# Fewer ones-matmuls in the RMS statistics, and residual adds as two wide VectorE operations

## The chip, the cores and the metric

The kernel runs on all eight cores of one Trainium2 chip, with the same program on each core and different tokens. The metric is device time in microseconds (us) of the slowest core. A run's time is some 2 us above its slowest core's span, so times are compared with times and spans with spans. The chip has two dies of four cores. In some executions of any version one die, or both, gets a lower TensorE clock. Such runs are called slow.

## The reference, cut to what matters

```python
def rmsnorm(x, g):
    xf = x.astype(jnp.float32)
    y = xf * lax.rsqrt(jnp.mean(xf * xf, axis=-1, keepdims=True) + EPS)
    return (y * g.astype(jnp.float32)).astype(x.dtype)

for i in range(DEPTH):                       # 4 layers
    h = rmsnorm(x, g[0]); x = x + 0.5 * rmsnorm(swiglu(h, ...), g[1])
    h = rmsnorm(x, g[2]); m = conv_mixer(h) if i % 2 == 0 else pool_mixer(h)
    x = x + rmsnorm(m, g[3])
    h = rmsnorm(x, g[4]); x = x + 0.5 * rmsnorm(swiglu(h, ...), g[5])
```

D_MODEL is 1024. Norms 0, 2 and 4 of a layer are prenorms, and norms 1, 3 and 5 are postnorms, each followed by a residual add.

## The kernel before

A core takes its 2112 tokens in two passes of three tiles (`t`) of 352 tokens. Model channels lie on the 128 partitions, so a tile is 8 chunks of 128 x 352. The mean over channels is therefore a sum across partitions. The kernel gets it by multiplying the squares with a 128 x 128 matrix of ones, 8 matmuls into one PSUM bank (PSUM is the memory, in eight banks here, that TensorE writes its sums to):

```python
def norm_stats(t, srcs, skeys, scale=None):
    b = t % 2
    v = S.vt(stat=True)                      # the one statistics bank
    for c in range(NCH):
        srcs(c, b)                           # ACT: sq[b][:, c, :] = square, bf16
    for hf in range(2):
        def f(pe, hf=hf):
            for c in range(4 * hf, 4 * hf + 4):
                mm = pe.matmul(B(v)[:, 0:TS], lhsT=ones_bf[:], rhs=sq[b][:, c, :], start=(c == 0), stop=(c == NCH - 1))
            return mm
        S.op("pe", f, 4 * MM, ...)
    S.op("act", [... Ln in the bank, then Exp(-0.5 *) into rr[b] ...])

def postnorm(l, n, t, half):
    ...
    for c in range(NCH):                     # scaling, in place, on VectorE
        S.op("dve", ... acc = acc * gain * rr ..., c_dve(TS) + 0.02, ...)
    for c in range(NCH):                     # residual add
        eng = "pool" if c < 4 else "dve"
        S.op(eng, ... x = x + acc ..., c_pool(TS) if eng == "pool" else c_dve(TS), ...)
```

`S.op` does not run anything. A list scheduler orders all operations beforehand: the third argument is a cost in us from a small table (`c_dve`, `c_act`, `c_pool`, `MM`), and each engine later executes its own list strictly in that order. If the table is wrong, an engine can stand before an operation whose input is late while others behind it are ready.

Of the kernel before, what the change touches and what calls it, by code (L numbers as in the profile page):

```python
# [12 lines left out]
D = 1024  # L13
# [378 lines left out]
def build_program():  # L392
# [19 lines left out]
    x = [sb(f"x{t}", [128, NCH, TS], F32) for t in range(NTILE)]  # L412
    h = [sb(f"h{t}", [128, NCH, TS], BF16) for t in range(NTILE)]
    acc = [sb(f"acc{t}", [128, NCH, ACW], F32) for t in range(NTILE)]
    sq = [sb(f"sq{i}", [128, NCH, TS], BF16) for i in range(2)]
    gt = [sb(f"gt{i}", [128, GRP, TS], BF16) for i in range(2)]
    ring = sb("ring", [128, RU, 1024], BF16)
    wdn = [sb(f"wdn{i}", [128, GRP * 128], BF16) for i in range(NCH)]
# [26 lines left out]
    def B(v):  # L445
        return banks[S.vbank[v]]
# [37 lines left out]
            st["ld"] += 1  # L484
        return units

    def norm_stats(t, srcs, skeys, scale=None):

        b = t % 2
        v = S.vt(stat=True)  # L490
        for c in range(NCH):
            srcs(c, b)
        for hf in range(2):
            def f(pe, hf=hf):
                for c in range(4 * hf, 4 * hf + 4):
                    mm = pe.matmul(B(v)[:, 0:TS], lhsT=ones_bf[:], rhs=sq[b][:, c, :], start=(c == 0), stop=(c == NCH - 1))
                return mm
            S.op("pe", f, 4 * MM, reads=["ones"] + [("sq", b, c) for c in range(4 * hf, 4 * hf + 4)], vts=[v],
                 prio=P_STAT, margin=0.6)
        S.op("act", [lambda a: a.activation(out=B(v)[:, 0:TS], in_=B(v)[:, 0:TS], func=AF.Ln, scale=1.0 / D, bias=epst[:, 0:1]),  # L500
                     lambda a: a.activation(out=rr[b][:], in_=B(v)[:, 0:TS], func=AF.Exp, scale=-0.5)],
             2 * c_act(TS) + 0.15, reads=["eps"], writes=[("rr", b)], vts=[v], prio=P_CH, margin=0.2, tbl="lnexp", wvt=True)

    def sq_sbuf(t, src, key, off):
        def s(c, b):
            S.op("act", lambda a: a.activation(out=sq[b][:, c, :], in_=src[:, c, off:off + TS], func=AF.Square),
                 c_act(TS, True), reads=[(key, t, c)], writes=[("sq", b, c)], prio=P_CH, margin=0.1)
        return s

    def prenorm(l, n, t, to_u=False):  # L510
        b = t % 2
        norm_stats(t, sq_sbuf(t, x[t], "x", 0), None)
        for c in range(NCH):
            g = gcol(l, n, c)
            dst = acc[t][:, c, PAD:ACW] if to_u else h[t][:, c, :]
            S.op("dve", lambda v, c=c, g=g, dst=dst: v.scalar_tensor_tensor(
                out=dst, in0=x[t][:, c, :], scalar=params[:, g:g + 1], in1=rr[b][:], op0=ALU.mult, op1=ALU.mult),
                c_dve(TS) + 0.02, reads=[("x", t, c), ("rr", b), "params"], writes=[("acc" if to_u else "h", t, c)],
                prio=P_CH, margin=0.1)

    def postnorm(l, n, t, half):
        b = t % 2
        pt = params_h if half else params
        pk = "params_h" if half else "params"
        for c in range(NCH):
            g = gcol(l, n, c)
            S.op("dve", lambda v, c=c, g=g: v.scalar_tensor_tensor(
                out=acc[t][:, c, PAD:ACW], in0=acc[t][:, c, PAD:ACW], scalar=pt[:, g:g + 1], in1=rr[b][:],
                op0=ALU.mult, op1=ALU.mult),
                c_dve(TS) + 0.02, reads=[("acc", t, c), ("rr", b), pk], writes=[("acc", t, c)], prio=P_CH, margin=0.1)  # L530
        for c in range(NCH):
            eng = "pool" if c < 4 else "dve"
            S.op(eng, lambda v, c=c: v.tensor_tensor(out=x[t][:, c, :], in0=x[t][:, c, :], in1=acc[t][:, c, PAD:ACW], op=ALU.add),
                 c_pool(TS) if eng == "pool" else c_dve(TS), reads=[("acc", t, c), ("x", t, c)], writes=[("x", t, c)],
                 prio=P_CH, margin=0.1)

    def ffn_tile(g, t, slots, finish):
        u = st["u"] % 2
        st["u"] += 1
        for jj in range(GRP):  # L540
            q = st["q"] % 3
            st["q"] += 1
            va, vb = S.vt(), S.vt()
            for v, un in ((va, slots[jj][0]), (vb, slots[jj][1])):
                def fa(pe, v=v, un=un):
                    for k in range(NCH):
                        mm = pe.matmul(B(v)[:, 0:TS], lhsT=ring[:, un, k * 128:(k + 1) * 128], rhs=h[t][:, k, :],
                                       start=(k == 0), stop=(k == NCH - 1))
                    return mm
                S.op("pe", fa, NCH * MM, reads=[("h", t, k) for k in range(NCH)] + [("ru", un)], vts=[v])  # L550
            S.op("act", lambda a, va=va, q=q: a.activation(out=sa[q][:], in_=B(va)[:, 0:TS], func=AF.Silu),
                 c_act(TS), writes=[("sa", q)], vts=[va], prio=P_EV, tbl="silu")
            S.op("dve", lambda v_, vb=vb, q=q, u=u, jj=jj: v_.tensor_tensor(
                out=gt[u][:, jj, :], in0=B(vb)[:, 0:TS], in1=sa[q][:], op=ALU.mult),
                c_dve(TS), reads=[("sa", q)], writes=[("g", u, jj)], vts=[vb], prio=P_EV)
        for dc in range(NCH):
            v = S.vt()

            def fo(pe, v=v, u=u, dc=dc):
                for jj in range(GRP):  # L560
                    mm = pe.matmul(B(v)[:, 0:TS], lhsT=wdn[dc][:, jj * 128:(jj + 1) * 128], rhs=gt[u][:, jj, :],
                                   start=(jj == 0), stop=(jj == GRP - 1))
                return mm
            S.op("pe", fo, GRP * MM, reads=[("g", u, jj) for jj in range(GRP)] + [("wdn", dc)], vts=[v])
            if g == 0:
                S.op("act", lambda a, v=v, dc=dc: a.activation(out=acc[t][:, dc, PAD:ACW], in_=B(v)[:, 0:TS], func=AF.Copy),
                     c_act(TS), writes=[("acc", t, dc)], vts=[v], prio=P_EV)
            else:
                S.op("dve", lambda v_, v=v, dc=dc: v_.tensor_tensor(
                    out=acc[t][:, dc, PAD:ACW], in0=B(v)[:, 0:TS], in1=acc[t][:, dc, PAD:ACW], op=ALU.add),  # L570
                    c_dve(TS), reads=[("acc", t, dc)], writes=[("acc", t, dc)], vts=[v], prio=P_EV)
        if g == 1:
            norm_stats(t, sq_sbuf(t, acc[t], "acc", PAD), None)
            finish(t)

    def ffn(f, finish):
        for g in range(2):
            slots = [load_units(wab[f, g * GRP + jj], 2) for jj in range(GRP)]
            for dc in range(NCH):
                S.op("pool", lambda p_, dc=dc, g=g: p_.dma_start(out=wdn[dc][:], in_=wd[f, g, dc]), 0.55,  # L580
                     writes=[("wdn", dc)], dma=f"wdn{dc}", nbytes=GRP * 128 * 256, prio=-1)
            for t in range(NTILE):
                ffn_tile(g, t, slots, finish)

    def s6(ap):
        return ap.rearrange("p (s k) -> p s k", k=6)
# [4 lines left out]
    def conv_tile(j, p, t, slots, finish):  # L591
# [61 lines left out]
                S.op("sp", lambda e: e.dma_start(out=cs_p[j], in_=convh[:, j].rearrange("p a b -> p (a b)")), 0.06,  # L653
                     reads=[("convh", j, c) for c in range(NCH)], dma="cs_p", nbytes=8192, final=True)

        def sqs(dc, b):
            v = S.vt()

            def fw(pe):
                for cc in range(NCH):  # L660
                    mm = pe.matmul(B(v)[:, 0:TS], lhsT=wdn[dc][:, cc * 128:(cc + 1) * 128], rhs=gt[u][:, cc, :],
                                   start=(cc == 0), stop=(cc == NCH - 1))
                return mm
            gk = [("g", u, cc) for cc in range(NCH)]
            S.op("pe", fw, NCH * MM, reads=gk + [("wdn", dc)], vts=[v])
            S.op("act", lambda a: a.activation(out=acc[t][:, dc, PAD:ACW], in_=B(v)[:, 0:TS], func=AF.Copy), c_act(TS),
                 writes=[("acc", t, dc)], vts=[v], prio=P_EV)
            S.op("act", lambda a: a.activation(out=sq[b][:, dc, :], in_=B(v)[:, 0:TS], func=AF.Square), c_act(TS),
                 writes=[("sq", b, dc)], vts=[v], prio=P_EV)
        norm_stats(t, sqs, None)  # L670
        finish(t)

    def conv_mixer(l, p, finish):
# [20 lines left out]
    def pool_tile(l, p, t, finish):  # L694
# [70 lines left out]
                        in1=Sv[:, c * NSS:(c + 1) * NSS, 15:19], op0=ALU.mult, op1=ALU.subtract), 0.2,  # L765
                        reads=[("wins", g % 2), "S0", "S1"], writes=[("h", t, c)], prio=P_CH)

        def sqs(dc, b):
            v = S.vt()
            g = dc // 2  # L770

            def fp(pe):
                for cc in range(2):
# [5 lines left out]
            sc = 240 + j * 8 + dc  # L779
            S.op("act", lambda a: a.activation(out=A[:, dc, PAD:ACW], in_=B(v)[:, 0:TS], func=AF.Copy, scale=params[:, sc:sc + 1]),  # L780
                 c_act(TS) + 0.09, reads=["params"], writes=[("acc", t, dc)], vts=[v], prio=P_EV)
            S.op("act", lambda a: a.activation(out=sq[b][:, dc, :], in_=B(v)[:, 0:TS], func=AF.Square, scale=params[:, sc:sc + 1]),
                 c_act(TS) + 0.09, reads=["params"], writes=[("sq", b, dc)], vts=[v], prio=P_EV)
        norm_stats(t, sqs, None)
        finish(t)

    def win_view(a0, w):
# [20 lines left out]
    for p in range(NPASS):  # L808
        for l in range(NLAYER):
# [3 lines left out]

            def fin1(t, l=l, p=p, conv=conv):
                postnorm(l, 1, t, True)
                prenorm(l, 2, t, to_u=not conv)
                if not conv:
                    pool_tile(l, p, t, fin2)

            def fin2(t, l=l):  # L820
                postnorm(l, 3, t, False)
                prenorm(l, 4, t)

            def fin3(t, l=l, p=p):
                postnorm(l, 5, t, True)
# [5 lines left out]
                        load_x(p + 1, t)  # L831
                        prenorm(0, 0, t)

            ffn(2 * l, fin1)
            if conv:
                conv_mixer(l, p, fin2)
            ffn(2 * l + 1, fin3)

    S.run()
    S.finish()  # L840
# [82 lines left out]
```

## Time and profile before

| | before |
|---|---|
| fast runs | 4532.48, 4532.67, 4533.64 us |
| TensorE busy | 4459.6 us, 98% |
| VectorE, ScalarE, GpSimd busy | 42%, 40%, 18% |
| matmuls | 29,760, of them 1152 with ones |

The views that matter are quoted in the prediction below. A line of the groups reads: source line, engine, operation, output<-inputs, shapes, count, then busy us and mean ns of one, then the idle time in front of it and what ended that. A line of busy time by stretch reads: stretch, its length, then busy us and count (x) for TensorE, its weight loads, VectorE, ScalarE and GpSimd, then granted clock, DMA share and GB/s. A line of the waits reads: who waited for whom, total us, times, longest.

In the names, `sq`, `sqf` and `sqs` are squares and their sums, `rr` is the result of the Exp, that is the norm's factor, and `h` is the output of a prenorm, which the next matmuls read.

To tell pace from loss I use one measure throughout: **lost** = length of a stretch minus its matmuls x 0.1491 us, the spacing in a steady stretch.

### The profile page before, as it was taken

The numbers are of one execution on the slowest core, as the hardware profiler recorded it, in microseconds if no ns is written. First come the engines' busy times: TensorE is split into PE (matmuls) and PEld (weight loads), VectorE is DVE, ScalarE is ACT, GpSimd is POOL, SyncE is SP. The second block draws the span as 40 slices with busy tenths as digits, with TensorE's granted clock in tenths as the row PEclk, the third lists the DMA queues.
The fourth block names the chain that finished last, engine by engine and source line by source line (L and its number), as shares of the span: only waits on it lengthen the run. The fifth ranks groups of instructions, "written<-read, shape, count | busy, mean of one in ns | idle before, by whom it ended". The sixth has DMA issues, their size and how long they took to land.

```text
span 4532.7 us, 70376 instructions; the slowest of 8 cores (4528.3 to 4532.7 us)
## 1 busy us (share of the span) xinstructions
PE 4459.6 (98%) x29760; PEld 2911.6 (64%) x29760; DVE 1926.4 (42%) x3581; ACT 1832.7 (40%) x3527; POOL 824.2 (18%) x1329
## 2 busy tenths in 40 slices
PE   7999999999999999999999999999999999999998
PEld 4666666666666666666666666666666666666665
DVE  2255151753336424174333642427342463342834
ACT  3345242553334424264333443426443444343632
POOL 1122020321112211032111221113111121111311
PEclk9999999999999999999999999999999999999999
DMA  6445444424444544443553444444444434444440
GB/s 126 73 75 89 77 77 77 68 44 69 65 77 68 89 77 77 77 77 52 102 108 65 68 84 77 77 77 77 74 68 65 66 56 77 74 77 77 82 74 39
DMA packets 104571, 340.10 MB, mean 75 GB/s; under 512 B 11840, under 2 KB 13248, under 8 KB 104256
## 3 DMA queue, kind: packets, MB, share of 16 engines
q0 software_dynamic: 97776, 312.52, 43.2%
q1 hardware_dynamic: 6480, 23.09, 1.6%
q8 instruction: 234, 3.83, 0.3%
q14 instruction: 81, 0.66, 0.1%
HBM read 636.49 MB, written 11.55 MB: 143 GB/s over the span
## 4 chain that ended last, share of the span: by engine, by line
PE 93%; DVE 4%; ACT 2%; DMA 1%; issue 0%; SPq 0%; DVEq 0%
PE ps L350 93%; DVE acc L350 2%; DMA x<-x_in 1%; ACT sq L350 1%; DVE x L350 1%; DVE gt L350 0%; ACT L350 0%; DVE h L350 0%; ACT ps L350 0%; ACT sa L350 0%; ACT rr L350 0%; DVE scr L350 0%; ACT acc L350 0%; SPq L350 0%; DVEq L368 0%
## 5 line engine op out<-in xcount | busy, mean ns | idle before, releaser
L350 PE MATMUL ps<-h,ring 128*128 128x352 bf16 x19200 | 2924.4, 313 | 0.0
L350 PEld LDWEIGHTS ps<-h,ring 128*128 128x128 bf16 x19200 | 1881.4, 98 | 990.7 <-DVE h L350 0.5
L350 PE MATMUL ps<-gt,wdn 128*128 128x352 bf16 x9216 | 1406.6, 313 | 1.1 <-DVE gt L350 0.8
L350 DVE TENSOR_TENSOR gt<-ps,sa 128x352 bf16<-128x352 f32 x1056 | 550.2, 522 | 1929.7 <-PE ps L350 1893.1
L350 PEld LDWEIGHTS ps<-gt,wdn 128*128 128x128 bf16 x9216 | 901.2, 98 | 475.6 <-DVE gt L350 2.9
L350 ACT ACTIVATE sa<-ps 128x352 f32<-128x352 f32 x1152 | 531.8, 462 | 1387.6 <-PE ps L350 1333.1
L350 POOL DMA_DIRECT2D ring<-wab x352 | 189.2, 539 | 1758.9 <-PE ps L350 1751.5
L350 POOL TENSOR_TENSOR x<-x,acc 128x352 f32<-128x352 f32 x288 | 323.6, 1146 | 979.9 <-DVE acc L350 979.2
L350 ACT ACTIVATE acc<-ps 128x352 f32<-128x352 f32 x480 | 222.6, 464 | 494.3 <-PE ps L350 494.3
L350 DVE TENSOR_TENSOR acc<-ps,acc 128x352 f32<-128x352 f32 x384 | 200.7, 523 | 454.3 <-PE ps L350 453.8
L350 ACT ACTIVATE sq<-acc 128x352 bf16<-128x352 f32 x384 | 190.7, 497 | 450.1 <-DVE acc L350 449.9
L350 ACT ACTIVATE sq<-x 128x352 bf16<-128x352 f32 x576 | 271.5, 494 | 190.5 <-DVE x L350 83.4
L350 DVE SCALAR_TENSOR_TENSOR acc<-acc,params_h,rr 128x352 f32<-128x352 f32 x384 | 312.1, 861 | 28.5 <-ACT rr L350 28.5
L350 ACT ACT_TABLE_LOAD x235 | 301.5, 1283 | 5.7 <-PEq L393 1.1
L350 PE MATMUL ps<-sq,ones_bf 128*128 128x352 bf16 x1152 | 223.0, 318 | 58.4 <-ACT sq L350 39.9
L350 DVE SCALAR_TENSOR_TENSOR h<-x,params_sb,rr 128x352 bf16<-128x352 f32 x480 | 254.6, 578 | 51.3 <-ACT rr L350 50.8
L350 POOL DMA_DIRECT2D wdn<-wd x256 | 135.7, 533 | 327.1 <-PE ps L350 327.1
L350 PEld LDWEIGHTS ps<-sq,ones_bf 128*128 128x128 bf16 x1152 | 110.5, 99 | 130.3 <-ACT sq L350 50.4
L350 DVE SCALAR_TENSOR_TENSOR acc<-acc,params_sb,rr 128x352 f32<-128x352 f32 x192 | 150.1, 827 | 7.7 <-ACT rr L350 7.7
L350 DVE TENSOR_TENSOR x<-x,acc 128x352 f32<-128x352 f32 x288 | 137.9, 512 | 0.0
L350 DVE SCALAR_TENSOR_TENSOR scr<-scr,params_sb 128x352 f32<-128x352 f32 (+1 forms) x192 | 117.8, 614 | 25.2 <-ACT scr L350 23.5
L350 ACT ACTIVATE scr<-scr,params_sb 128x352 f32<-128x352 f32 (+1 forms) x96 | 57.0, 594 | 120.4 <-DVE scr L350 120.4
(39 smaller groups left out, 833.4 us busy)
## 6 DMA issues: line engine op xcount, KB each, us to landing
ring<-wab POOLq DMA_DIRECT2D x352, 512.0 KB, 11.3
wdn<-wd POOLq DMA_DIRECT2D x256, 352.0 KB, 15.8
ring<-wci POOLq DMA_DIRECT2D x29, 768.0 KB, 11.4
x<-x_in SPq DMA_DIRECT2D x12, 704.0 KB, 12.4
y_o<-x SPq DMA_DIRECT2D x12, 704.0 KB, 4.0
wdn<-wco POOLq DMA_DIRECT2D x32, 256.0 KB, 12.9
scr<-spool SPq DMA_DIRECT2D x4, 608.0 KB, 13.0
ps_s<-scr SPq DMA_DIRECT2D x4, 608.0 KB, 2.9
```

The source lines that it names most:

```text
L350: ins = attr(*a, **k)
```

## The change

The intent is to take matmuls off the bound engine. Squares are kept in fp32 and VectorE adds 8 chunks to 2, so that two ones-matmuls do. It is used wherever the statistic can come later without harm: in all norms of the convolution layers, and in norms 0 and 5 of the pooling layers. The four middle norms of the pooling layers keep eight matmuls. Separately, the residual adds leave GpSimd and become two adds of 1408 columns on VectorE.

```diff
-    sq = [sb(f"sq{i}", [128, NCH, TS], BF16) for i in range(2)]
+    sqf = sb("sqf", [128, NCH, TS], F32)         # one buffer; sq[0], sq[1] become views of it
+    sqs2 = sb("sqs", [128, 2, TS], BF16)
...
+    def norm_stats_pre(t, srcs):
+        for hf in range(2):
+            srcs(hf)                             # ACT: one square of 4 chunks, 1408 columns
+            o = 4 * hf
+            S.op("dve", ... sqf[:, o:o + 2] += sqf[:, o + 2:o + 4] ..., c_dve(2 * TS), ...)
+        S.op("dve", ... sqs2 = sqf[:, 0:2] + sqf[:, 4:6] ..., c_dve(2 * TS), ...)
+        def f(pe):
+            for c in range(2):
+                mm = pe.matmul(B(v)[:, 0:TS], lhsT=ones_bf[:], rhs=sqs2[:, c, :], start=(c == 0), stop=(c == 1))
+            return mm
...  # postnorm
-        for c in range(NCH):
-            eng = "pool" if c < 4 else "dve"
-            S.op(eng, ... x[t][:, c, :] + acc[t][:, c, PAD:ACW] ...)
+        for hf in range(2):
+            o = 4 * hf
+            ... four scalings of acc ...
+            S.op("dve", ... x[t][:, o:o + 4, :] + acc[t][:, o:o + 4, PAD:ACW] ..., c_dve(4 * TS), ...)
...
-                prenorm(l, 2, t, to_u=not conv)
+                prenorm(l, 2, t, to_u=not conv, pre=conv)
...
-            ffn(2 * l + 1, fin3)
+            last = p == NPASS - 1 and l == NLAYER - 1
+            ffn(2 * l + 1, fin3, lambda t, last=last: not (last and t == NTILE - 1))
```

## The prediction

> **What bounds the kernel now.** I read the busy table first, then the groups of instructions, then busy time by stretch, then the waits of TensorE, then the order of time inside one troubled stretch. The busy table and the groups come first:
>
> ```profile
> PE 4459.6 (98%) x29760; PEld 2911.6 (64%) x29760; DVE 1926.4 (42%) x3581; ACT 1832.7 (40%) x3527; POOL 824.2 (18%) x1329
> ...
> L350 POOL TENSOR_TENSOR x<-x,acc 128x352 f32<-128x352 f32 x288 | 323.6, 1146 | 979.9 <-DVE acc L350 979.2
> ...
> L350 DVE SCALAR_TENSOR_TENSOR acc<-acc,params_h,rr 128x352 f32<-128x352 f32 x384 | 312.1, 861 | 28.5 <-ACT rr L350 28.5
> ...
> L350 PE MATMUL ps<-sq,ones_bf 128*128 128x352 bf16 x1152 | 223.0, 318 | 58.4 <-ACT sq L350 39.9
> ...
> L350 DVE SCALAR_TENSOR_TENSOR h<-x,params_sb,rr 128x352 bf16<-128x352 f32 x480 | 254.6, 578 | 51.3 <-ACT rr L350 50.8
> ```
>
> TensorE is busy 98% of the span, everything else under half. 1152 of its 29,760 matmuls are the ones-matmuls of the norm statistics (144 norms of 8), so they cost the path directly. The mean of 318 ns is of a pipelined instruction; the price is the spacing, which I take from busy time by stretch (columns: stretch, length, then busy time and count for each engine, then granted clock, DMA share, GB/s):
>
> ```profile
> 256.00:622.00 366.00, 365.93 (x2454) 240.05 (x2455) 167.59 (x322) 151.01 (x296) 73.68 (x142) 1.00 0.46 73
> 943.00:1372.00 429.00, 428.98 (x2877) 281.21 (x2875) 153.98 (x286) 160.50 (x305) 62.94 (x91) 1.00 0.41 66
> 1977.00:2053.00 76.00, 69.80 (x459) 43.99 (x457) 63.96 (x106) 52.58 (x100) 32.36 (x40) 1.00 0.72 115
> 2053.00:2063.00 10.00, 9.34 (x52) 5.66 (x53) 7.42 (x13) 6.72 (x10) 1.95 (x2) 0.83 0.01 2
> 3092.00:3170.00 78.00, 71.45 (x474) 45.60 (x471) 64.80 (x107) 51.98 (x100) 33.08 (x41) 1.00 0.69 112
> ```
>
> 429.00 / 2877 = 0.1491 us per matmul in a steady stretch, and 366 / 2454 gives the same. 29,760 x 0.1491 = 4437 us, so 96 us of the 4532.7 are not matmuls at full pace. I can place them. Up to 38 us only 34 matmuls are done (33 us lost, a little more while the clock recovers); the end, from 4517 us, holds 7 (15 us lost). The pooling layers, two in each of two passes, show as four stretches of 76 to 78 us, which lose most of the rest: 76 - 459 x 0.1491 = 7.6 us here, 7.3 to 7.8 in the others, 30 us in all, and about 1.6 us more each while the clock is down after the last gap (52 matmuls in 10 us at a granted 0.83), some 6 us. So 36 us are pooling-layer stalls; some 10 us are scattered over the rest. In them VectorE is busy 64 of 76 us.
>
> TensorE's own waits name the cause:
>
> ```profile
> PE ps L350 <- ACT sq L350: 39.9, 23, 11.4
> PE ps L350 <- ACT rr L350: 18.4, 13, 3.1
> PE ps L350 <- DVE gt L350: 0.8, 2, 0.6
> ```
>
> It hardly ever waits for anything but ones-matmuls: for their squares, or for the one statistics bank that the previous Exp still reads. The kernel fixes its instruction order beforehand from a table of costs; it puts a ones-matmul where that table says its input is ready, and other matmuls were free to take the place. So such a wait is mostly an error of the table. The order of time in the second pooling stretch shows the error:
>
> ```profile
> 1978.47 6.75 DVE L350 SCALAR_TENSOR_TENSOR acc<-acc,params_sb,rr 128x352 f32<-128x352 f32 x8 [0.52 <-ACT rr L350]
> ...
> 1995.38 1.38 DVE L350 TENSOR_TENSOR x<-x,acc 128x352 f32<-128x352 f32 x3
> 1996.69 1.56 DVE L350 SCALAR_TENSOR_TENSOR h<-x,params_sb,rr 128x352 bf16<-128x352 f32 x3
> ```
>
> ```profile
> 1979.14 4.71 POOL L350 TENSOR_TENSOR x<-x,acc 128x352 f32<-128x352 f32 x4 [0.92 <-DVE acc L350]
> ```
>
> Eight scalings of acc take 6.75 us while GpSimd adds beside them; undisturbed ones follow each other every (1.56 - 0.57) / 2 = 0.49 us, so eight should take 4.0. The table knows 0.54 each and no such slowing.
>
> **What the Trainium skill says.** "TensorE: Matmul & The Clock Gate", "Wait — 56ns, not 53.3ns?": a warm matmul of N columns costs N / 2.4 ns + 2.5, for 352 columns 149.2 ns. The trace's 149.1 agrees. "SBUF — State Buffer", "SBUF: two separate sides": VectorE with two SBUF inputs and a GpSimd operation that reads SBUF exclude each other on a shared port pair for the whole instruction. The 6.75 us for eight agree. "VectorE: DVE Perf Modes", "The TRN2 errata": an fp32 two-tensor add takes (N + 151) / 0.96 ns, for 352 columns 524; the trace has 512. "ScalarE: Activation LUTs", "What ACT_TABLE_LOAD costs": an activation with immediates takes 186 + 0.833 N ns and successive ones overlap by 93; 479 for 352, and the trace has 494 to 497 for the squares.
>
> **The change, part by part.** Statistics first. Which norms change: in the convolution layers all 6, in the pooling layers the first and the last; 8 per pair of layers, times 2 pairs, 2 passes and 3 tiles makes 96, and the last tile of all is left out: 95. Each goes from 8 ones-matmuls to 2, so 95 x 6 = 570 matmuls go. All lie in streams where TensorE is full, so **570 x 0.1491 = 85.0 us** come off the path. Nothing of what replaces them is on TensorE.
>
> What it adds to VectorE: three fp32 adds of 704 columns. An undisturbed add of 352 repeats every (1.38 - 0.51) / 2 = 0.435 us, that is 352 / 0.96 GHz = 0.367 plus 0.068; for 704 columns 0.80, estimated. 95 x 3 x 0.80 = 228 us, beside the matmuls. ScalarE gets cheaper where it squares from SBUF: two wide instructions of about 1.36 us by the skill's formula for eight at a spacing near 0.39. The statistic comes some 2 us later than before (a wide square and two adds after the last chunk instead of one small square). In the convolution layers a tile has the time of other tiles' matmuls to finish, 264 x 0.149 = 39 us each, so I count 0 for that.
>
> Residual adds. Per postnorm (72 of them) VectorE before: 6.75 + 4 x 0.435 = 8.5 us, with GpSimd's 4.7 beside it. After: 8 x 0.49 + 2 x (1408 / 960 + 0.068) = 3.9 + 3.1 = 7.0 us, nothing on GpSimd. So the move takes 1.5 us of VectorE away per postnorm. In total: 72 x 1.5 = 108 less, 228 more, so VectorE goes from 1926 to about 2045 us, 45%.
>
> What this is worth on the path: the pooling layers keep their 8 ones-matmuls in the middle norms, so only the residual part reaches those stretches. It takes about 6 x 1.5 = 9 us of VectorE work out of 76, and the table's 8.2 us (0.54 each plus two adds of 1.62, and small gaps) is then above the real 7.0 instead of below the real 8.5. Waits that are errors of the table should mostly go. GpSimd's windowed sums still disturb VectorE there, so not all: I take **22 of the 36 us**.
>
> Start: tile 2's statistics become one step later in TensorE's order, not two halves with the first blocking; 0 to 4 us, I take **2**. End: the last tile keeps the old statistics, then 7.1 us of VectorE replace 8.5: **1.3**.
>
> Sum: 4532.7 - 85.0 - 22 - 2 - 1.3 = 4422 us.
>
> **Rivals.** (a) Only the matmuls count: the pooling waits are real shortage, or new order errors replace the old. Then 4532.7 - 85 - 1 = 4447 us, just inside 2%. For it: VectorE is still the busiest engine there. Against: each gap ends at a ones-matmul while plenty of other matmuls follow at once. (b) VectorE becomes the bound: adds of 1.5 us and 228 us of new work delay evictions, TensorE waits for banks, and the saving is eaten: 4470 to 4530. For it: the longest new operation outlasts one matmul group of 8 (1.2 us). Against: seven banks for it, and VectorE at 42% overall. (c) All pooling stalls go, and the start gains 4: 4532.7 - 85 - 36 - 5 = 4407. (d) The longer statistics chain stalls TensorE in the convolution layers, 1 us for each of 95 norms: the gain shrinks to about 4510; the 39 us of slack per tile speak against it.
>
> **Range and chances.** The 85 us are a count and nearly sure. What is open is 0 to 36 us of stalls, with (b) and (d) unlikely. So 4407 to 4443. The 2% line is 4442; only near-total failure of the second part crosses it: faster 0.87, same 0.12, slower 0.01.
>
> **What would show it.** TensorE with 29,190 matmuls, 582 of them ones-matmuls, still 0.149 us apart; acc scalings at a mean near 0.57 us instead of 0.83 to 0.86; no GpSimd adds of x; adds of 704 columns near 0.87 us each, of 1408 near 1.6; TensorE's waits for squares and Exp down from 58 us to about 30, with most of that at the start; pooling stretches losing 2 to 4 us each. It is wrong if the pooling stretches still lose 7 us, if TensorE waits for VectorE's sums in the convolution layers, or if its matmul spacing changes.

## The result, and the profile after

| | before | after |
|---|---|---|
| fast runs, us | 4532.48, 4532.67, 4533.64 | 4414.52, 4415.19 |
| slow runs, us | 4747.26 | 4499.20, 4754.77 |
| median of all four, us | 4533.16 | 4457.19 |
| span of the profiled run, us | 4532.7 | 4412.7 |

The ratio is 0.974, with a 95% interval of 0.9711 to 0.9768. A ratio is the mean time of one kernel's fast runs over that of the other's of the same rounds, so it is not quite the ratio of the medians; here the medians also contain slow runs. The changed kernel is 118 us faster.

First the busy table and the groups of the changed kernel:

```profile
PE 4360.3 (99%) x29190; PEld 2855.3 (65%) x29190; DVE 2090.1 (47%) x3722; ACT 1728.4 (39%) x3021; POOL 510.7 (12%) x1041
...
L350 DVE TENSOR_TENSOR x<-x,acc 128x1408 f32<-128x1408 f32 x144 | 232.9, 1617 | 0.9
L350 DVE SCALAR_TENSOR_TENSOR acc<-acc,params_h,rr 128x352 f32<-128x352 f32 x384 | 200.5, 579 | 52.2 <-ACT rr L350 52.2
L350 DVE TENSOR_TENSOR sqf<-sqf 128x704 f32<-128x704 f32 x190 | 165.8, 885 | 66.4 <-ACT sqf L350 66.0
```

There are 29,190 matmuls, 570 fewer. The scalings of acc take 579 ns in place of 861, with the same shape and the same count. VectorE has grown to 47%.

Busy time by stretch, a steady stretch and the second and third pooling stretches:

```profile
256.00:622.00 366.00, 366.00 (x2456) 240.06 (x2455) 198.73 (x361) 146.60 (x248) 53.08 (x125) 1.00 0.50 78
1925.00:1998.00 73.00, 70.82 (x472) 45.94 (x472) 58.72 (x98) 52.97 (x103) 14.76 (x23) 1.00 0.70 112
1998.00:2008.00 10.00, 9.66 (x65) 6.38 (x66) 9.68 (x19) 3.83 (x10) 2.20 (x3) 1.00 0.01 2
3018.00:3090.00 72.00, 69.81 (x466) 45.28 (x467) 58.67 (x99) 49.75 (x99) 14.69 (x23) 1.00 0.71 111
```

The steady pace is unchanged: 366 / 2456 = 0.149 us. The second pooling stretch now loses 73 - 472 x 0.1491 = 2.6 us where it lost 7.6, and in the 10 us behind it the clock stays at 1.00 where it had been 0.83.

The waits of TensorE:

```profile
PE ps L350 <- DVE sqs L350: 19.1, 2, 17.3
PE ps L350 <- ACT rr L350: 10.2, 8, 1.4
PE ps L350 <- DVE h L350: 8.8, 2, 8.3
PE ps L350 <- ACT sqf L350: 1.1, 1, 1.1
```

The two waits for VectorE's sums (sqs) are both at the start, before 43 us, and so is the long wait for h. In the whole rest of the run TensorE never waits for the new sums. Of the waits for squares, 39.9 us in 23 before, one is left. For the reading of all the runs below it matters that 29.1 of those 39.9 us, in 5 waits, lie in the first 44 us; the rest of the run, nearly all of it in the pooling layers, has the other 10.7 us, in 18, besides the 18.4 us for rr.

In order of time, one postnorm in the second pooling stretch:

```profile
1926.03 2.57 DVE L350 SCALAR_TENSOR_TENSOR acc<-acc,params_h,rr 128x352 f32<-128x352 f32 x5 [2.29 <-ACT rr L350]
1928.65 0.52 DVE L350 TENSOR_TENSOR gt<-ps,sa 128x352 bf16<-128x352 f32 x1
1929.09 1.62 DVE L350 TENSOR_TENSOR x<-x,acc 128x1408 f32<-128x1408 f32 x1
```

Five scalings take 2.57 us, one every (2.57 - 0.58) / 4 = 0.50 us; GpSimd started nothing between 1923.5 and 1928.9 us.

Where the 120 us between the spans come from, by lost time. A pooling layer is counted as its stretch together with the 10 us behind it:

| part | before | after | gain |
|---|---|---|---|
| 570 matmuls at 0.1491 | | | 85.0 |
| four pooling layers, lost | 37.7 | 10.2 | 27.5 |
| first 44 us, lost | 35.5 | 31.0 | 4.5 |
| end, from the last group of projections on | 15.4 | 14.4 | 1.0 |
| everything else, lost | 4 | 2.4 | 1.5 |
| sum | | | 119.5 |

A matmul that crosses a boundary is counted in both windows. This hides some 3 us of loss before and 2.4 after, so the gains are good to about 0.5 us.

### The profile page after: what moved, and what is told of

It is laid out like the page before. It is cut to its first block, busy times and chain, and to the rows that moved or that the text cites. A ratio compares the mean times of both kernels' runs of the same rounds, so it can differ in the third digit from the quotient of the medians.

```text
span 4412.7 us, 68624 instructions; the slowest of 8 cores (4411.6 to 4412.7 us)
## 1 busy us (share of the span) xinstructions
PE 4360.3 (99%) x29190; PEld 2855.2 (65%) x29190; DVE 2089.8 (47%) x3722; ACT 1730.8 (39%) x3021; POOL 510.7 (12%) x1041
## 4 chain that ended last, share of the span: by engine, by line
PE 98%; DMA 1%; ACT 1%; DVE 0%; SPq 0%; issue 0%; DVEq 0%
PE ps L350 98%; DMA x<-x_in 1%; ACT sqf L350 0%; ACT L350 0%; ACT ps L350 0%; DVE acc L350 0%; ACT rr L350 0%; SPq L350 0%; DVE x L350 0%; ACT sa L350 0%; DVE gt L350 0%; DVE sqs L350 0%; DVE sqf L350 0%; DVEq L362 0%
## 5 line engine op out<-in xcount | busy, mean ns | idle before, releaser
L350 ACT ACTIVATE sqf<-acc 128x352 bf16<-128x352 f32 (+1 forms) x174 | 148.0, 852 | 476.8 <-DVE acc L350 464.2
L350 ACT ACTIVATE sqf<-x 128x352 bf16<-128x352 f32 (+1 forms) x288 | 213.6, 783 | 72.3 <-DVE x L350 51.1
L350 DVE TENSOR_TENSOR x<-x,acc 128x1408 f32<-128x1408 f32 x144 | 232.8, 1617 | 0.9
L350 DVE SCALAR_TENSOR_TENSOR acc<-acc,params_h,rr 128x352 f32<-128x352 f32 x384 | 200.5, 578 | 52.3 <-ACT rr L350 52.3
L350 DVE TENSOR_TENSOR sqf<-sqf 128x704 f32<-128x704 f32 x190 | 165.7, 885 | 66.3 <-ACT sqf L350 66.0
L350 DVE SCALAR_TENSOR_TENSOR acc<-acc,params_sb,rr 128x352 f32<-128x352 f32 x192 | 103.3, 577 | 9.0 <-ACT rr L350 9.0
L350 POOL TENSOR_TENSOR scr<-acc 128x352 f32<-128x352 f32 (+3 forms) x48 | 48.2, 1012 | 425.3 <-DVE acc L350 365.4
L350 DVE TENSOR_TENSOR sqs<-sqf 128x704 bf16<-128x704 f32 x95 | 84.2, 886 | 1.5
## 6 DMA issues: line engine op xcount, KB each, us to landing
wdn<-wco POOLq DMA_DIRECT2D x32, 256.0 KB, 14.2
```

Of the source, the lines that this page charges most:

```text
L350: ins = attr(*a, **k)
```

## The experiments

My theory had two halves: the matmuls count at their full pace, and the pooling stalls are errors of order, made by a table that does not know that GpSimd's adds slow VectorE down. The main rivals were that the stalls were a real shortage of VectorE, and that width was what helped. Eleven kernels ran, in four groups, each group on one chip. All gave correct results. Kernels of one group share their runs of the kernel before. In the first two groups all of those were slow; in the other two the fast ones took 4532.80 to 4534.09 us, the same as above. In the first two groups the dies of the kernel before that kept their clock end at spans of 4527 to 4533 us, so it stood at the same place there, and I take 4533 us for it throughout. One kernel of a group can so stand against one of another group, on another chip; where the difference is small, this is a weakness.

### The statistics alone

```diff
# the changed kernel, with postnorm() of before
-        for hf in range(2): ... four scalings, one add of 1408 columns on VectorE
+        for c in range(NCH): ... scaling; then per chunk an add, c < 4 on GpSimd
```

> The statistics part alone: 570 ones-matmuls fewer, residual adds as before (four of eight on GpSimd). If the two parts are independent, as the prediction has them: 4532.7 - 85.0 for the matmuls - 4.5 at the start, with the pooling stretches still losing about 9 us each, so 4443 us (4438 to 4448), ratio 0.980. If the pooling stalls fell because of the statistics part, it would come near 4415.

Measured: fast runs 4441.88, 4442.77 and 4443.41 us. The waits of TensorE on its slowest core:

```profile
PE ps L350 <- ACT rr L350: 18.1, 12, 3.1
PE ps L350 <- ACT sqf L350: 9.9, 14, 1.4
```

The statistics part brings 90 us, as expected: the matmuls and the start. It leaves the pooling waits as they were. The waits for Exp (rr) are 18.1 us in 12, against 18.4 in 13 before, those for squares 9.9 us in 14 against 10.7 in 18 after the start; the four pooling layers lose 39 us, against 38 before.

### The residual adds alone

```diff
# the kernel before, with postnorm() of the changed kernel
```

> The residual part alone: scalings and two adds of 1408 columns on VectorE, no GpSimd add; statistics as before, 29,760 matmuls. By the theory the pooling stretches lose some 2.5 us each in place of 9.4: 4532.7 - 27.5 - 1 = 4504 us (4498 to 4510). By the rival that only the ones-matmuls count: 4532.

Measured: fast runs 4504.80 and 4505.02 us, so 28 us faster with not one matmul less. The waits of TensorE:

```profile
PE ps L350 <- ACT sq L350: 29.4, 6, 12.5
PE ps L350 <- ACT rr L350: 11.7, 10, 1.4
```

All but 1.1 us of the first line lie at the start; the pooling layers lose 11.5 us. The two parts add up: 90 + 28 = 118. The rival that only the ones-matmuls count is out.

### Off GpSimd, but narrow

```diff
-            eng = "pool" if c < 4 else "dve"
+            eng = "dve"
```

> Before, with the four GpSimd adds moved to VectorE as narrow adds, so eight adds of 352 columns and nothing wide. Tells apart GpSimd's disturbance and width. If the disturbance is the cause, the scalings of acc fall from 861 and 827 to about 578 ns and the time is within 4 us of the residual part alone, about 4504 to 4508. If the width (fewer instructions) is what counts, it stays above 4520.

Measured: fast runs 4503.62, 4503.78 and 4504.55 us. The group of scalings:

```profile
L350 DVE SCALAR_TENSOR_TENSOR acc<-acc,params_h,rr 128x352 f32<-128x352 f32 x384 | 202.8, 578 | 35.5 <-ACT rr L350 35.5
```

This one-word edit brings all that the wide adds bring; it is even 1 us ahead. The width is worth nothing here. What helps is that GpSimd no longer adds beside the scalings. That the load is not the point shows in VectorE's busy time: 1894 us here and 1865 with the wide adds, 29 us more for the same time.

### The same instructions, a truer table

```diff
# the kernel before; only the costs that the scheduler uses in postnorm
-                c_dve(TS) + 0.02, ...                     # scaling: 0.54 us
+                0.84, ...
-                 c_pool(TS) if eng == "pool" else ...      # GpSimd add: 0.95 us
+                 1.16 if eng == "pool" else ...
```

> Before, with no instruction changed, only the cost table that fixes the order: a scaling in the postnorm 0.84 us in place of 0.54, a GpSimd add 1.16 in place of 0.95, as the trace has them. If the pooling waits are errors of the table, most go although VectorE has as much work and GpSimd disturbs it as much: 4505 to 4518. If they are a real shortage of VectorE, the time stays at 4530 or more.

Measured: fast runs 4512.47, 4512.94 and 4514.10 us. The groups of the scalings and the GpSimd adds, then the waits of TensorE:

```profile
L350 POOL TENSOR_TENSOR x<-x,acc 128x352 f32<-128x352 f32 x288 | 306.7, 1083 | 945.1 <-DVE acc L350 943.5
L350 DVE SCALAR_TENSOR_TENSOR acc<-acc,params_h,rr 128x352 f32<-128x352 f32 x384 | 291.7, 799 | 40.3 <-ACT rr L350 40.3
```

```profile
PE ps L350 <- ACT sq L350: 28.0, 6, 11.1
PE ps L350 <- ACT rr L350: 12.6, 11, 1.7
```

GpSimd still adds, and the scalings are still slow at 799 ns. Still 20 us went. TensorE's waits for squares fell from 23 to 6, after the start from 10.7 us in 18 to 1.1 in one, and those for rr from 18.4 us to 12.6. The four pooling layers lose 16 us in place of 38, so 22 us came back there; some 5 us went anew between 2065 and 3080 us, where TensorE waits once, for 2.7 us, for weights from a DMA. So most of the gain of the residual part is a gain of order: the instructions were not too much work, they stood in the wrong place. The other 4 us that the pooling layers lose beyond the two runs above may be real slowness of VectorE or other wrong entries; this run does not part them.

### The changed kernel, a table that is too low

```diff
# the changed kernel; only the costs in postnorm
-                    c_dve(TS) + 0.02, ...     # scaling: 0.54 us
+                    0.36, ...
-                 c_dve(4 * TS), ...           # wide add: 1.62 us
+                 1.20, ...
```

> The changed kernel, no instruction changed, only its cost table made too low where the residual part is ordered: a scaling in the postnorm 0.36 us in place of 0.54 (the trace: 0.49), a wide add 1.20 in place of 1.62 (the trace: 1.54), so a postnorm 5.3 us for a real 7.0. If the pooling waits come from a table below the truth, TensorE waits again for squares and for the Exp in the pooling stretches: 4424 to 4440, ratio 0.976 to 0.980. If only the real load of VectorE counts, it stays at 4415.

Measured: one undisturbed run of 4439.79 us. Another, at 4461.44: two of its cores were at a clock of 0.991; in four slow runs, three dies that kept their clock end at spans of 4433.5 to 4437.6. The waits of TensorE on core 0 of the profiled run, which is of such a die (span 4436.5):

```profile
PE ps L350 <- ACT rr L350: 19.5, 12, 4.4
...
PE ps L350 <- ACT sqf L350: 6.2, 7, 1.1
```

The same instructions lose 25 us of the 28 again, through order alone: the pooling layers lose 31 us, where the changed kernel loses 10. This is the mirror of the run before it, and the rival of a real shortage in the kernel before falls for the larger part. No run changed the table at random, so how far an order that is merely different moves the time is not known; but all three edits of the table, this one, the one before and the last of all, moved it to the side and by the amount that I had written down.

### The shorter statistics in the pooling layers too

```diff
-                prenorm(l, 2, t, to_u=not conv, pre=conv)
+                prenorm(l, 2, t, to_u=not conv)
-                prenorm(l, 4, t, pre=conv)
+                prenorm(l, 4, t)
-            ffn(2 * l, fin1, lambda t, conv=conv: conv)
+            ffn(2 * l, fin1)
# and in pool_tile: squares into sqf, then norm_stats_pre
```

> The changed kernel with the shorter statistics in the middle norms of the pooling layers too (47 or 48 more norms, 6 ones-matmuls each; only the last tile keeps eight). 48 x 6 x 0.149 = 43 us fewer matmuls. If the 115 us of extra VectorE sums (48 x 2.4) fit beside them: 4372. In these stretches VectorE is already at 59 of 73 us and 12 norms x 2.4 = 29 us come on top, so 88 us for 73: by this the chain of VectorE becomes the bound there and each stretch grows by 8 to 15 us instead: 4400 to 4435. I expect the second, 4405 to 4430.

Measured: all six runs were slow. In each of four of them one die kept its state and ended at spans of 4541 to 4545 us (its mean clock of 0.982, the same on all four, I take as its own, from the gaps below, where the clock is 0.79). That is some 131 us worse than the changed kernel's span and well outside what I expected. The waits of TensorE on core 4, of such a die:

```profile
PE ps L350 <- DVE sqs L350: 126.9, 14, 16.8
PE ps L350 <- DVE h L350: 59.5, 14, 8.3
```

Busy time in the emptiest 40 us of the first pooling layer, core 4, and a line of the order of time from it:

```profile
900.00:940.00 40.00, 22.41 (x138) 13.68 (x137) 23.15 (x37) 21.78 (x35) 0.00 (x0) 0.79 0.00 1
```

```profile
925.18 1.38 ACT L350 ACTIVATE sqf<-acc 128x1408 f32<-128x1408 f32 x1 [1.89 <-DVE sqs L350]
```

VectorE, which I had named as the bound, is busy only 23 of 40 us, and no engine more than that: they wait for each other. The line shows what happens: the squares of one tile wait until VectorE has made the last sum of another tile. `sqf` is a single buffer, and in the pooling layers one tile needs it four times in a row, so the next tile cannot begin. I took this as a new theory and tested it.

### Two buffers of bf16 squares in all layers

```diff
-    sqf = sb("sqf", [128, NCH, TS], F32)
+    sq = [sb(f"sq{i}", [128, NCH, TS], BF16) for i in range(2)]     # tile t uses sq[t % 2]
# three in-place bf16 adds, then two ones-matmuls on sq[b][:, 0:2], in every norm but the last tile's
```

(Two fp32 buffers, which would have changed the buffer alone, were not run; the next experiment takes the other way.)

> The shorter statistics in all layers but with squares in bf16 in two buffers (one for even, one for odd tiles) instead of one fp32 buffer for all, and the three adds in bf16. The fp32 version in all layers took 4543 us on its undisturbed die, with TensorE waiting 127 us for sums and 60 us for h. Theory: the one buffer made the three tiles' chains run one after the other, since VectorE was busy only 23 of 40 us in the emptiest stretch. Then two buffers free them: the matmuls of all 143 norms fall from 8 to 2, 4532.7 - 143 x 6 x 0.149 - 33 = 4372 us if nothing else stalls, 4372 to 4400 with some stalls. Rival: VectorE's extra sums in the pooling layers, then 4450 or more. The adds should also show whether bf16 halves them, 887 to about 500 ns; if they do, VectorE's load is less as well and the two causes are not fully parted by this run alone. Rounded sums may miss the accuracy bound; expected correct.

Measured: fast runs 4419.15, 4419.37 and 4420.27 us, ratio 0.975 (0.9726 to 0.9773). The group of the adds, then the waits of TensorE:

```profile
L350 DVE TENSOR_TENSOR sq<-sq 128x704 bf16<-128x704 bf16 x429 | 221.4, 521 | 150.4 <-ACT sq L350 146.8
```

```profile
PE ps L350 <- DVE h L350: 42.7, 12, 8.3
PE ps L350 <- DVE sq L350: 17.4, 1, 17.4
```

The sums cost TensorE nothing beyond the start any more, but it now waits 12 times for h, and 288 matmuls fewer than the changed kernel's bring no gain. Of the 42.7 us for h, 30.5 in 10 waits come after the first 44 us. I read this as a real limit in the pooling layers: the chain of a tile from one feed-forward block to the next is too long to be hidden. It is not shown. The table's entry that the last run finds wrong stands in this version too, and no run parts a limit from a wrong order here. The adds run at 521 ns for 704 columns where fp32 needs 885, in line with the two-fold bf16 rate that the Trainium skill gives two-tensor operations ("VectorE: DVE Perf Modes", "The perf-mode tier table").

### The same with a single buffer

```diff
-        q = sq[b]
+        q = sq[0]
# and likewise where the squares are written
```

> The all-layers version with bf16 squares and sums (4419 to 4420 us), with one of its two buffers of squares used for all three tiles. Parts the two differences to the fp32 all-layers version (4543 us on an undisturbed die). If the single buffer chains the tiles: 4525 to 4550 on an undisturbed die, TensorE waiting over 100 us for sums. If the width of the sums was what counted: 4420.

Measured: one fast run, 4514.82 us (a second was slow), on another chip than the run before it. The waits of TensorE:

```profile
PE ps L350 <- DVE sq L350: 103.2, 14, 17.5
PE ps L350 <- DVE h L350: 51.8, 10, 8.0
```

The buffer alone is worth 95 us, which settles the larger cause. The time lies below the range that I had written, so the buffer is not all: from the spans, about 4543 - 4512 = 31 us are left. The likely rest is that bf16 sums take 521 ns and fp32 ones 885, but the two versions also differ in where the last sum goes (in place, or to `sqs`), and this was not parted.

### One or four ones-matmuls, in bf16

```diff
# bf16 squares in two buffers, as above
-        for c in range(2): ... two matmuls on the summed chunks
+        # one matmul, after a fourth add, where the changed kernel has two;
+        # four matmuls, after two adds, in the middle norms of the pooling layers
```

> As the run with bf16 squares in two buffers, but one ones-matmul where the changed kernel has two, and four, after only two narrow adds, in the middle norms of the pooling layers. Matmuls: 95 x 7 + 48 x 4 = 857 fewer than before, 128 us; 4532.7 - 128 - 33 = 4372 if nothing stalls, and less risk of stalls in the pooling layers than two matmuls there. 4370 to 4390. By the rival that the pooling layers hold no further sums: above 4402, the changed kernel with one ones-matmul.

Measured: fast runs 4404.08 and 4407.07 us, ratio 0.9718 (0.9695 to 0.9742). A wait of TensorE on core 4, of a die that kept its clock:

```profile
PE ps L350 <- DVE h L350: 28.5, 10, 8.6
```

Against the next run it has 192 matmuls fewer, worth 28.6 us. Of the waits for h, 17.7 us in 8 come after the first 44 us, so the pooling layers lose the larger part of what they save in such waits; the rest is not placed. The time is above that of the next run, so the theory's range was wrong and its rival right.

### One ones-matmul in the changed kernel

```diff
-            for c in range(2):
-                mm = pe.matmul(..., rhs=sqs2[:, c, :], start=(c == 0), stop=(c == 1))
+            # after one more add, sqs2[:, 0] = sqf[:, 0] + sqf[:, 1]
+            return pe.matmul(..., rhs=sqs2[:, 0, :], start=True, stop=True)
```

> The changed kernel with the two summed chunks added once more, so one ones-matmul per changed norm: 95 x 0.149 = 14.2 us fewer matmuls for 95 x 0.435 = 41 us more of VectorE. If the convolution layers have the slack that the prediction gives them: 4400 to 4402, ratio to the changed kernel 0.997. If the longer chain begins to hold TensorE: no gain or a loss, 4414 or more.

Measured: one undisturbed run of 4402.14 us. Two more, 4432.77 and 4445.12, had cores at clocks of 0.988 to 0.994; their undisturbed cores end at 4399 to 4403, those of the first at 4398 to 4401, where the changed kernel's end at 4411 to 4414. The gain is nearly 13 us of the 14.2 that the 95 matmuls are worth.

### One more entry of the table put right

```diff
# prenorm() of the version with one ones-matmul
-                c_dve(TS) + 0.02, reads=[("x", t, c), ("rr", b), "params"], ...
+                0.70 if to_u else c_dve(TS) + 0.02, reads=[("x", t, c), ("rr", b), "params"], ...
```

> The changed kernel with one ones-matmul, and one entry of its cost table corrected: a prenorm scaling into acc in the pooling layers 0.70 us, as its mean in the trace, in place of 0.54. If the remaining 10 us of pooling stalls are again errors of the table: 4394 to 4399 against 4402. If they come from the order of Ln and Exp on ScalarE: no change, 4402.

Measured: fast runs 4396.58, 4396.85 and 4396.85 us. TensorE's waits for the Exp fell from 10.2 us in 8 to:

```profile
PE ps L350 <- ACT rr L350: 5.6, 4, 1.7
```

A cost entry, not an instruction, was worth another 5.4 us, between two groups on two chips; the pooling layers lose 5 us, where they lost 11 without it. This version beats both kernels: 136 us below before and 18 below the changed kernel.

## Why the prediction was right, point by point

**The matmuls.** Counted at 570 x 0.1491 = 85.0 us, and found: 29,190 matmuls at the same spacing. The statistics alone gave 90 us, with about 5 of them from the start.

**The pooling stalls.** The mechanism was right and is shown twice, by the truer table in the kernel before and the too low one in the changed kernel. The size was taken too small: 22 of 36 us foretold, 27.5 of 37.7 measured. The 36 itself was a little low: I put the first pooling stretch at no more than 7.8 us, from pieces whose borders count a matmul twice, and read whole it loses 77 - 458 x 0.1491 = 8.7. The share of 22 was a guess. I had expected GpSimd's windowed sums to keep more of the stalls; about 10 us stay, and the last run shows that half of those are an error of the table again. Nor is the new table above the truth by as much as I said: its entries for a postnorm add up to 7.5 us (8.2 with gaps, as I had it), against 7.5 measured, so it is about true.

**The residual part's work on VectorE.** Its saving was over-sized. I foretold 1.5 us per postnorm. The groups give (312.1 + 150.1 + 137.9) / 72 = 8.3 us before and (200.5 + 103.4 + 232.9) / 72 = 7.5 after, 0.9 less. I had priced operations at the spacing of a back-to-back row, but evictions break these rows up. For the same reason the sums cost 250 us instead of 228, and VectorE is at 2090 us instead of 2045. It did not matter for the time, since little of the saving acts through load: of the two reasons for the 22 us, 9 us less work in each stretch and a truer table, the runs bear out the second.

**The slack in the convolution layers.** It was counted as 0 cost and was: no wait for sums after the start.

**Start and end.** 2 and 1.3 us were foretold, 4.5 and 1.0 measured. In the first 44 us 81 other matmuls pass where 33 did; with the statistics alone 84 pass, with the residual part alone 36, so it is the statistics. That their single step, later in the order, is the reason was foretold and not tested. All in all the forecast of 4422 us was a span, and the span is 4412.7: the gains foretold add up to 110 us and 120 came, nearly all of the difference from the stalls (5.5) and the start (2.5).

**The rivals.** Rival (a), 4447 us, is what the statistics alone came to (4442), and the residual part carried the result past it. Rival (b), VectorE as the bound, and rival (d), longer chains in the convolution layers, show nothing: VectorE is named in no wait of TensorE after the start but one of 0.6 us. What I had not thought of is the cost of a buffer: the change avoids it only by leaving the middle norms of the pooling layers alone.

## What to carry to other kernels

Where a fixed order is made from a cost table, look at the waits of the bound engine first: if it waits for one kind of operation while others stand ready behind it, correct the table entry by the trace before moving any work. An entry measured alone need not hold beside another engine (here 0.54 us in the table, 0.83 to 0.86 in the trace), so take the mean from the trace, not from a formula. Work that replaces bound work needs not only a free engine but also free buffers: with one shared buffer three tiles waited for each other, and in the emptiest 40 us no engine was busy for more than 23.

## What the Trainium skill lacked or had wrong

- "SBUF — State Buffer", "SBUF: two separate sides": it says that the loser of the shared ports blocks fully, but gives no figure for what a row of such operations loses. Here eight scalings beside four GpSimd adds took 6.75 us in place of 4.0, so each add of about 1.15 us took some 0.7 us from VectorE.
- "TensorE: Matmul & The Clock Gate", "Back-to-back issue gap": its figure for a real stream, about 131 ns at 512 columns, does not fit a stream of weight loads and matmuls that needs 149.1 ns at 352; the page's other formula, N / 2.4 + 2.5, does.
- The same page, "Seeing it yourself": it advises to budget 13/16 of the clock for dense matmuls on all cores. The fast runs of the two kernels here had 0.996 to 0.999 on all eight cores over 4.4 to 4.5 ms. In slow runs the cores of a disturbed die had mean clocks from 0.98 down to 0.81, so here the 13/16 looks like the lower end of a state that comes and goes, not like a constant. The page speaks of the default power profile; which one this chip had is not on record.
- No page speaks of an instruction order fixed beforehand from a cost table. Here two entries of such a table were worth 20 to 25 us of 4.5 ms.
